# Router logits of the second mixture layer: tokens streamed over a stationary router, additions ahead of the turns, low parts behind the choice

## The chip, the cores and the metric

One Trainium2 chip, one of its cores. The time is that of one execution on the device in microseconds, the median of several runs. The core has TensorE (matmuls, "PE" in the rows, with its weight loads as "PEld"), VectorE ("DVE"), ScalarE ("ACT"), GpSimd ("POOL") and SyncE ("SP", which issues the DMAs here).

## What is computed

Two layers of a transformer over 512 tokens of width 1024. Layer 0 is attention and a mixture of experts, layer 1 a pooling mixer and a mixture of experts; a last norm ends it. The change lies between the pooling mixer of layer 1 and its mixture. There the reference does, in float32:

```python
x_lat = x_lat + g_m * pool_mixer(h_l, ...)          # four channel groups of 256, windows 2, 4, 8, 16
tokens = modulate(rms_norm(x_lat, norm_ffn_g[i]), sh_f, sc_f)
pg = softmax(tokens @ w_rg)                          # 4 groups
le = tokens @ w_re                                   # 32 experts, 8 of them per group
grp = top_k(pg, 1); two experts = top_k(le of that group, 2)
y = for each chosen expert: (silu(h @ w_gate) * (h @ w_up)) @ w_down, weighted and summed per token
```

So each token needs 36 logits (4 + 32), a choice from them, its rank among the tokens of its expert, and then the experts' products, two experts (a pair) at a time, for which 16 pairs of weights of 12 MB each are streamed from HBM.

## The kernel before, in words

Tokens lie on partitions, in NT = 4 tiles of 128; `x(j)` is token tile j, 1024 channels wide, or 8 chunks of 128 channels (k = 0 to 7). The program fixes the order of every engine's instructions by the order in which the code issues them; a tile pool adds the waits when a buffer is used again. PSUM is handed out by tags: one bank each for "g", "u", "t" and "ga", two for "y" and two for "c"; the router's bias takes a "y" bank, the logits bank `self.lg` the "ga" bank.

`pool_layer` (L1680) does the pooling. For each channel group g of 256 channels (two chunks), `project(g, tags)` (L1756) multiplies the pooled differences by the group's weights: 16 matmuls of TensorE into two banks. `added(g, ps)` (L1770) adds each bank to `x` on VectorE (two token tiles at once) and then squares the sums on ScalarE, one activation with a running sum for each token tile. When a chunk k of `x` is final, `turn(k, tag, eng)` (L1782) transposes it: four transposes on TensorE into a PSUM bank, then a copy into `xT` by ScalarE or VectorE. The chunks that are final first are turned first: 0, 1 (group 0), 6, 7 (group 3), 4, 5 (group 2) and 2, 3 (group 1).

`logits(*ks)` (L1791) multiplies the turned chunks by the router. The turned 128 tokens are the stationary operand, 128 columns of the router (36 of them the chunk's logits, the rest what lies behind) the moving one: four products per chunk, 32 in all, which add up in the bank `self.lg`. A matmul with zeros opens that bank.

The norm's factor r is not needed for the products: `add_shift` (L1180) multiplies the logits by r and adds the bias `bw`. It comes from `ss`, the 16 sums of squares per token: a sum, `rstd_of` (L501: a square root on ScalarE and five small steps on VectorE, with a place for other work between them, the argument `fill`). With r, `norm_high` (L1161) writes the rounded half `hi` of a normed token tile on ScalarE, and `norm_low` (L1169) the rest `lo` on VectorE, in two pieces for each token tile j, one for the even and one for the odd chunks.

Behind the logits stand `choose` (L1198, some 24 small VectorE steps that end in the table `M`), on TensorE meanwhile `row_bcast` (L477) and `zeros` (L1337, 20 matmuls with zeros that open four banks), then `rank` (L1239), `one_hot_tile` (L1552, the table `OH` of slots for token tile j) and `gather_part` (L1344), which for a pair of chunks and some token tiles multiplies `hi` and `lo` (parts 0 and 1) by `OH`: 64 matmuls altogether. ScalarE and VectorE evict them into `xe` (L1353). Then every engine passes a branch (`overflow`, L1495: taken if an expert has more tokens than it has slots), and the mixture runs (`moe`, L1563), pair after pair. Its weights come through `Stream` (L117), a ring of 12 buffers that `fill` issues on SP and `done` gives back.

Of the kernel before, what the change touches and what calls it, by code (L numbers as in the profile page):

```python
# [11 lines left out]
F32 = mybir.dt.float32  # L12
# [4 lines left out]
ALU = mybir.AluOpType  # L17
AX = mybir.AxisListType.X
PSUM = bass.MemoryType.PSUM

D = 1024
KD = D // 128
SEQ = 512
NT = SEQ // 128
# [3 lines left out]
HD = 64  # L28
# [4 lines left out]
NE = 32  # L33
NG = 4
# [5 lines left out]
UNIT = 64  # L40
# [26 lines left out]
_C = {}  # L67
_off = 0
for _n, _w in (("ident", 128), ("iota", SEQ), ("tcol", NT), ("w8", EPG), ("w4", NG),
               ("islot", UNIT), ("edge", 4 * 16), ("tri", 128), ("cos", NT * HD), ("sin", NT * HD),  # L70
               ("band", sum(WB for WB in BANDS.values()))):
    _C[_n] = (_off, _off + _w)
    _off += _w
# [3 lines left out]
def make_consts():  # L77
    c = np.zeros((128, NCONST), np.float32)

    def put(n, v):  # L80
        a, b = _C[n]
        c[:, a:b] = v

    p = np.arange(128)
    put("ident", np.eye(128))
    put("tri", p[:, None] < p[None, :])
    put("iota", np.arange(SEQ)[None] + 1)

    put("islot", np.where(np.arange(UNIT) < CAP, np.arange(UNIT) + 1, 0.5)[None])
    put("tcol", p[:, None] + 128 * np.arange(NT)[None] + 1)  # L90
    put("w8", EPG - np.arange(EPG)[None])
    put("w4", NG - np.arange(NG)[None])
    t = np.r_[np.arange(8), np.arange(SEQ - 8, SEQ)]
    edge = [np.float32(w) / (np.minimum(t + w // 2, SEQ) - np.maximum(t - w // 2, 0)).astype(np.float32) for w in WINDOWS]
    put("edge", np.concatenate(edge)[None])
    nf = HD // 4
    inv = (np.float32(10000.0) ** (-np.arange(nf, dtype=np.float32) / np.float32(nf))).astype(np.float32)
    tok = np.arange(SEQ)
    ang = np.concatenate([(tok // GRID_W).astype(np.float32)[:, None] * inv,
                          (tok % GRID_W).astype(np.float32)[:, None] * inv], axis=1).astype(np.float32)  # L100
    cs = np.repeat(np.cos(ang), 2, axis=1).reshape(NT, 128, HD).transpose(1, 0, 2)
    sn = np.sin(ang)
    sn = np.stack([-sn, sn], axis=-1).reshape(NT, 128, HD).transpose(1, 0, 2)
    bands = []
    for w, z in BANDS:
        tile = (0, 1, NT - 1)[z]
        src = 128 * tile + np.arange(128)[:, None]
        t = max(0, 128 * tile - w // 2 + 1) + np.arange(BANDS[w, z])[None]
        lo, hi = np.maximum(t - w // 2, 0), np.minimum(t + w // 2, SEQ)
        bands.append(((src >= lo) & (src < hi)) * (np.float32(1) / (hi - lo).astype(np.float32)))  # L110
    put("band", np.concatenate(bands, axis=1))
    put("cos", cs.reshape(128, -1))
    put("sin", sn.reshape(128, -1))
    return c
# [82 lines left out]
class Kernel:  # L197
# [47 lines left out]
    def load_consts(self):  # L245
        nc, a, cp = self.nc, self.a, self.cp
        ca = _C["edge"][1]
        self.cst = cp.tile([128, ca], F32, name="cst")
        rows = self.rowsA = cp.tile([96, 128], F32, name="rowsA")
        nc.sync.dma_start(self.cst[:, :128], a["consts"][:, :128])  # L250
        for i, n in enumerate(("c", "c_ctx")):
            nc.sync.dma_start(rows[8 * i:8 * i + 8], a[n].rearrange("(k p) -> k p", p=128))
        self.xc = self.big([128, NC_, D], F32, "xc")
        nc.sync.dma_start(self.xc, a["ctx"].rearrange("(j p) d -> p j d", p=128))
        nc.sync.dma_start(rows[16:32], a["norm_mix_g"].rearrange("i (k p) -> (i k) p", p=128))
        nc.sync.dma_start(rows[32:48], a["norm_ffn_g"].rearrange("i (k p) -> (i k) p", p=128))
        nc.sync.dma_start(rows[48:96], a["b_ada"][0].rearrange("(k p) -> k p", p=128))
        g = lambda n: self.cst[:, _C[n][0]:_C[n][1]]
        self.ident, self.iota, self.islot = g("ident"), g("iota"), g("islot")
        self.tcol, self.w8, self.w4, self.edge = g("tcol"), g("w8"), g("w4"), g("edge")  # L260
        self.tri_b = cp.tile([128, 128], BF16, name="tri_b")
        self.ones_b = cp.tile([128, 128], BF16, name="ones_b")
        nc.vector.memset(self.ones_b, 1.0)
        self.ones = cp.tile([128, 32], F32, name="ones")
        nc.vector.memset(self.ones, 1.0)

        self.cols = cp.tile([128, 144], F32, name="cols")

        self.AB = {}

        self.AB2 = {}

        self.gates = cp.tile([128, 512], F32, name="gates")
        nc.gpsimd.memset(self.gates, 0.0)
# [1405 lines left out]
    def pool_layer(self, norms):  # L1680
        nc, mp, pm, st, sm, pw = self.nc, self.mp, self.pm, self.st, self.sm, self.pw
# [6 lines left out]
        zero = self.tri_b[:, 0:1].to_broadcast([128, 128]), self.ones_b[:, 0:1].to_broadcast([128, 512])  # L1688
# [67 lines left out]
        def project(g, tags):  # L1756

            ps = []
            for jj in range(2):
                p = pm.tile([128, 2, 256], F32, tag=tags[jj], name="pp")  # L1760
                for j in range(2):
                    for z in range(2):
                        nc.tensor.matmul(p[:, j], diff[2 * g + z][:, (2 * jj + j) * 128:(2 * jj + j + 1) * 128],
                                         pw[:, 2 * g + z], start=(z == 0), stop=(z == 1))
                ps.append(p)
            return g, ps

        ss = sm.tile([128, NT, 4], F32, name="ss16")

        def added(g, ps):  # L1770

            q = slice(g * 256, (g + 1) * 256)
            for jj in range(2):
                xs = self.xt[jj][:, :, q]
                nc.vector.tensor_add(xs, xs, ps[jj])
                for j in (2 * jj, 2 * jj + 1):
                    junk = mp.tile([128, 256], F32, name="act")
                    nc.scalar.activation(junk, self.x(j)[:, q], AF.Square, accum_out=ss[:, j, g:g + 1])

        xT = []  # L1780

        def turn(k, tag, eng):  # L1782

            if not xT:
                xT.extend(self.big([128, 4, 512], F32, "xT") for _ in range(2))
            p = pm.tile([128, 512], F32, tag=tag, name="pb")
            for j in range(NT):
                nc.tensor.transpose(p[:, j * 128:(j + 1) * 128], self.x(j)[:, k * 128:(k + 1) * 128], self.ident)
            (nc.scalar.copy if eng is nc.scalar else nc.vector.tensor_copy)(xT[k // 4][:, k % 4], p)

        def logits(*ks):  # L1791

            for k in ks:
                for j in range(NT):
                    nc.tensor.matmul(self.lg[:, j * 128:(j + 1) * 128], xT[k // 4][:, k % 4, j * 128:(j + 1) * 128], self.wr(k),
                                     start=False, stop=(k == 3 and j == NT - 1))

        for js in (range(2), range(2, NT)):
            for k in (0, 1, 6, 7):
# [29 lines left out]
        summed(3)  # L1829
        self.router(1, self.gw[:, 1])  # L1830
        self.norm_begin()
        nc.tensor.matmul(self.lg, *zero, start=True, stop=False)
        p2 = project(2, ("t", "y"))
        added(*p3)
        turn(0, "c", nc.scalar)
        turn(1, "c", nc.scalar)
        p1 = project(1, ("g", "u"))
        added(*p2)
        turn(6, "y", nc.scalar)
        turn(7, "c", nc.vector)  # L1840
        added(*p1)
        turn(4, "y", nc.vector)
        turn(5, "c", nc.vector)
        logits(0, 1, 6, 7)
        st4 = sm.tile([128, NT], F32, name="ss4")
        nc.vector.tensor_reduce(st4, ss, axis=AX, op=ALU.add)
        r = self.rstd_of(st4, NT, D, "n4")
        hl = {}

        def high(j):  # L1850
            hl[j] = self.norm_high(j, r[:, j:j + 1])

        def low(j, k):
            self.norm_low(j, r[:, j:j + 1], *hl[j], k)

        turn(2, "y", nc.vector)
        turn(3, "c", nc.scalar)
        high(0)
        high(1)
        logits(4, 5, 2, 3)  # L1860
        low(0, 0)
        low(0, 1)
        low(1, 0)
        low(1, 1)
        self.route_begin()
        for j in range(NT):
            self.add_shift(j, r[:, j:j + 1])
# [10 lines left out]
        OH = mp.tile([128, NT, 4 * CAP], F32R, name="OH")  # L1878
        for j in range(2):
            self.one_hot_tile(OH, 0, j)  # L1880
        self.fullest_of()
        for j in range(2, NT):
            self.one_hot_tile(OH, 0, j)
# [1 line left out]
                low(j, k)  # L1885
        self.spread_two()
        xe = self.slots_tile()
        for js in (range(2), range(2, 3)):
            for k in range(0, KD, 2):
                self.gather_part(OH, k, js)  # L1890
        self.tc.mark_branch_hint_location("over1", engines=(mybir.EngineType.PE,))
        for k in range(0, KD, 2):
            self.gather_part(OH, k, range(3, 4))
# [67 lines left out]
```

## Time and profile before

| what | value |
|---|---|
| median of 3 runs | 1376.76 us (1374.62 to 1382.63) |
| the profiled execution, its own time | 1378.12 us |
| its span, from the first to the last instruction | 1376.3 us |
| mean granted clock of TensorE | 0.987 of full speed |
| PE, DVE, ACT busy over the span | 96%, 48%, 26% |
| bytes read from HBM | 472.51 MB, 345 GB/s over the span |

The times in the rows are microseconds from the span's first instruction. Shares of busy time over the whole span say little here, since the change touches some 25 of 1376 us; the rows below are of that stretch, of the stretch behind it, and of a few other places where something alike was done.

### The profile page before, as it was taken

To read this page: it belongs to the slowest core of one execution; us is meant where nothing else is said; L and a number is where in the kernel's file an instruction comes from. 1 tells how busy PE (TensorE), PEld (TensorE's weight loads), DVE (VectorE), ACT (ScalarE), POOL (GpSimd) and SP (SyncE) were. 2 spreads that over 40 slices of the span, in tenths; PEclk is the share of its full clock that TensorE was granted. 3 is DMA by queue.
4 is the path that set the end of the run, shared out by engine and by line. 5 is a ranking of instruction groups with operands and counts; after the bars stand their busy time and mean duration, and the time that the engine had idled before them with its cause. 6 is when DMAs were issued, how large, how long until landed. Compare 5 with 4: busy or idle time off the path is not lost. (4 is left out here: it accounts for less than half of the span.)

```text
span 1376.3 us, 18679 instructions
## 1 busy us (share of the span) xinstructions
PE 1314.4 (96%) x7191; PEld 736.4 (54%) x7191; DVE 659.7 (48%) x1290; ACT 363.7 (26%) x707; POOL 130.2 (9%) x130
## 2 busy tenths in 40 slices
PE   3799999999999999999999999999999999999995
PEld 1578677778744544445444435754455444554442
DVE  2778788867823434234342335744234342343335
ACT  2554687763311111111111105521111111111103
POOL 1523344340000000000000010000000000000001
PEclk9799999999999999999999999999999999999998
DMA  9411846159489999999999999579999999999994
GB/s 373 171 62 62 337 142 227 40 197 361 191 365 426 427 426 427 426 427 426 426 427 426 422 411 423 225 292 411 426 426 427 425 427 426 427 426 426 427 420 172
DMA packets 80704, 475.91 MB, mean 346 GB/s; under 512 B 8512, under 2 KB 10064, under 8 KB 30432
## 3 DMA queue, kind: packets, MB, share of 16 engines
q1 hardware_dynamic: 80600, 474.64, 84.0%
q8 instruction: 58, 0.95, 0.3%
q14 instruction: 38, 0.31, 0.1%
q10 hardware_dynamic: 8, 0.01, 0.0%
HBM read 472.51 MB, written 2.11 MB: 345 GB/s over the span
## 5 line engine op out<-in xcount | busy, mean ns | idle before, releaser
L1371 PE MATMUL pgate<-wt,xe 128*64 128x512 f32 x1024 | 273.1, 593 | 2.7 <-ACTq L1504 2.1
L1371 PE MATMUL pup<-wt,xe 128*64 128x512 f32 x1024 | 271.8, 592 | 0.3 <-DVEq L1504 0.3
L1396 PE MATMUL py<-wt,aT 128*64 128x512 f32 x960 | 212.6, 595 | 0.0
L1376 DVE TENSOR_TENSOR act<-act,pup 128x512 f32<-128x512 f32 x32 | 22.0, 689 | 342.8 <-ACT act L1375 310.5
L1427 DVE TENSOR_TENSOR x<-x,pc 128x512 f32<-128x512 f32 x240 | 154.1, 683 | 29.9 <-PE pc L1425 29.9
L1371 PEld LDWEIGHTS pgate<-wt,xe 128*64 128x64 f32 x1024 | 75.8, 137 | 148.5 <-issue 129.5
L1371 PEld LDWEIGHTS pup<-wt,xe 128*64 128x64 f32 x1024 | 76.5, 137 | 145.5 <-issue 143.2
L1425 PE MATMUL pc<-y,scat 128*128 128x512 f32 x480 | 136.7, 406 | 2.4 <-DVE x L1427 2.4
L1409 DVE SCALAR_TENSOR_TENSOR py<-py,r_sw,gw 128x512 f32<-128x512 f32 x64 | 48.6, 759 | 178.4 <-PE py L1396 169.5
L1396 PEld LDWEIGHTS py<-wt,aT 128*64 128x64 f32 x960 | 66.9, 137 | 124.0 <-issue 118.8
L1325 PE MATMUL pga<-OH,xnp 128*128 128x224 f32 x896 | 119.3, 277 | 0.0
L1325 PEld LDWEIGHTS pga<-OH,xnp 128*128 128x128 f32 x896 | 114.3, 191 | 8.5 <-issue 1.6
L1375 ACT ACTIVATE act<-pgate 128x512 f32<-128x512 f32 x32 | 19.1, 597 | 360.8 <-PE pgate L1371 348.4
L1425 PEld LDWEIGHTS pc<-y,scat 128*128 128x128 f32 x480 | 80.3, 189 | 42.8 <-ACT act L1375 24.3
L1410 ACT ACTIVATE y<-py 128x512 fp32r<-128x512 f32 x64 | 38.1, 596 | 235.3 <-PE py L1396 160.1
L1334 POOL MEMSET xe<- 128x64 f32 x16 | 2.4, 151 | 781.6 <-PE pup L1371 551.3
L1360 ACT ACTIVATE xe<-pga,mod 128x224 f32<-128x224 f32 x64 | 33.8, 538 | 154.8 <-PE pga L1325 139.6
L562 PE MATMUL pmm<-whl,hT 128*128 128x512 f32 x288 | 70.6, 402 | 0.0
L850 DVE TENSOR_REDUCE mx<-S 128x1 f32<-128x768 f32 x64 | 58.3, 951 | 19.5 <-PE S L847 18.9
L562 PEld LDWEIGHTS pmm<-whl,hT 128*128 128x128 f32 x288 | 54.6, 193 | 11.3
L857 ACT ACTIVATE P<-S,mx 128x768 f32<-128x768 f32 x64 | 56.9, 899 | 2.2 <-POOL rest L731 2.1
L867 PE MATMUL PT<-cst,P 128*128 128x128 f32 x384 | 54.5, 277 | 0.1
(345 smaller groups left out, 1414.7 us busy)
## 6 DMA issues: line engine op xcount, KB each, us to landing
wt<-in_moe_w_gate_up_dram SPq DMA_DIRECT2D x224, 1024.0 KB
wt<-in_moe_w_down_dram SPq DMA_DIRECT2D x120, 1024.0 KB
wt<-in_w_ada_dram SPq DMA_DIRECT2D x48, 1024.0 KB
wt<-in_moe_w_gate_up_dram SPq DMA_DIRECT2D x64, 512.0 KB
wt<-in_moe_w_down_dram SPq DMA_DIRECT2D x16, 512.0 KB
wt<-in_attn_w_qkv_dram SPq DMA_DIRECT2D x6, 1024.0 KB
x<-in_x_dram SPq DMA_DIRECT2D x8, 512.0 KB
wt<-in_attn_w_o_dram SPq DMA_DIRECT2D x4, 1024.0 KB
```

The costliest lines, as they stand in the source:

```text
L562: self.nc.tensor.matmul(p, lhs(pa, k), whl[pb, k // 4][:, k % 4], start=(k + n == 0), stop=(k == KD - 1 and n == 2))
L850: nc.vector.tensor_reduce(m, s[:, :NKEY], axis=AX, op=ALU.max, negate=True)
L857: nc.scalar.activation(P[n][:, g], S.pop((n, g))[:, :NKEY], AF.Exp, bias=mx[n, g], accum_out=total[n // 4][:, 2 * gp + g, kvl:kvl + 1])
L867: nc.tensor.transpose(pt[:, cc, g * 128:(g + 1) * 128], P[n][:, g, c * 128:(c + 1) * 128], self.ident)
L1325: nc.tensor.matmul(p[:, :n], self.parts[part][j // 2][:, j % 2, k * 128:(k + 1) * 128], OH[:, j], start=(z == 0), stop=(z == 2 * NT - 1))
L1360: nc.scalar.activation(xe, p, AF.Identity, bias=B[:, k:k + 1], scale=A[:, k:k + 1])
L1371: nc.tensor.matmul(p[64 * e:64 * e + 64], xe(k)[:, offs[e]:offs[e] + UNIT], w[e][:, h * 512:(h + 1) * 512], start=(k == 0), stop=(k == KD ...
L1396: nc.tensor.matmul(py[h][64 * e:64 * e + 64], aT[:, j, 64 * e:64 * e + 64], wd[e][:, h * 512:(h + 1) * 512], start=(j == 0), stop=(j == 3) ...
L1409: nc.vector.scalar_tensor_tensor(py, py, w, gf[:, h * 512:(h + 1) * 512], op0=ALU.mult, op1=ALU.mult)
L1410: nc.scalar.activation(y[:, 0], py, AF.Copy)
L1425: nc.tensor.matmul(p, P[:, j * 128:(j + 1) * 128], y[:, part], start=(part == 0), stop=(part == 1))
L1427: nc.vector.tensor_add(xs, xs, p)
```

## The change: what it does

1. **Logits turned round.** The router's columns of a chunk (64 of them, 36 used) become the stationary operand, the 512 turned tokens the moving one. Even chunks go to the lower 64 columns of the array and to partitions 0 to 63 of one PSUM bank, odd chunks to the upper 64 and partitions 64 to 127: 8 products of 64x512. The bank then holds two halves of the sum, turned. `logits_end` copies it to SBUF (VectorE) and multiplies each 128 tokens of it by a constant table `halves` (a 1 where p mod 64 is the column), which turns it back and adds the halves: four products of 128x36 into `self.lg`. The matmul with zeros goes. The constants grow by 36 columns.
2. **Banks.** The bank of those halves is "t", so group 2's projection takes ("y", "y") in place of ("t", "y").
3. **Additions first.** Group 1's additions (`added(*p1)`) stand ahead of the turns of chunks 6 and 7, and the sum of squares and the norm's factor ahead of chunks 4 and 5, whose turns and the first logits are the work inside `rstd_of`. Copies change engine: 6 and 2 and 7 by VectorE, 4, 5 and 3 by ScalarE. `high(0)` stands ahead of the turns of 2 and 3.
4. **Low parts behind the choice.** Of the four `low` pieces of token tiles 0 and 1 that stood ahead of the choice one stays, behind `logits_end`; three go behind the first two `one_hot_tile`. The gather of token tiles 0 and 1 takes part 0 for all chunks first, and then part 1.

```diff
         def logits(*ks):
             for k in ks:
-                for j in range(NT):
-                    nc.tensor.matmul(self.lg[:, j * 128:(j + 1) * 128], xT[k // 4][:, k % 4, j * 128:(j + 1) * 128], self.wr(k),
-                                     start=False, stop=(k == 3 and j == NT - 1))
+                q = slice(k % 2 * 64, k % 2 * 64 + 64)
+                nc.tensor.matmul(lgT[0][q], self.wr(k)[:, :64], xT[k // 4][:, k % 4], start=(k < 2), stop=(k in (2, 3)),
+                                 tile_position=(0, k % 2 * 64))
+
+        def logits_end():
+            t = mp.tile([128, 512], F32, tag="aT", name="lgT")
+            nc.vector.tensor_copy(t, lgT[0])
+            for j in range(NT):
+                nc.tensor.matmul(self.lg[:, j * 128:j * 128 + NG + NE], t[:, j * 128:(j + 1) * 128], self.halves, start=True, stop=True)
...
-        nc.tensor.matmul(self.lg, *zero, start=True, stop=False)
-        p2 = project(2, ("t", "y"))
+        lgT.append(pm.tile([128, 512], F32, tag="t", name="lgT"))
+        p2 = project(2, ("y", "y"))
         added(*p3)
         turn(0, "c", nc.scalar)
         turn(1, "c", nc.scalar)
         p1 = project(1, ("g", "u"))
         added(*p2)
-        turn(6, "y", nc.scalar)
+        added(*p1)
+        turn(6, "y", nc.vector)
         turn(7, "c", nc.vector)
-        added(*p1)
-        turn(4, "y", nc.vector)
-        turn(5, "c", nc.vector)
-        logits(0, 1, 6, 7)
         st4 = sm.tile([128, NT], F32, name="ss4")
-        nc.vector.tensor_reduce(st4, ss, axis=AX, op=ALU.add)
-        r = self.rstd_of(st4, NT, D, "n4")
...
+        nc.vector.tensor_reduce(st4, ss, axis=AX, op=ALU.add)
+
+        def meanwhile():
+            turn(4, "y", nc.scalar)
+            turn(5, "c", nc.scalar)
+            logits(0, 1, 6, 7)
+
+        r = self.rstd_of(st4, NT, D, "n4", meanwhile)
+        high(0)
         turn(2, "y", nc.vector)
         turn(3, "c", nc.scalar)
-        high(0)
         high(1)
         logits(4, 5, 2, 3)
+        logits_end()
         low(0, 0)
-        low(0, 1)
-        low(1, 0)
-        low(1, 1)
+        lows = [(0, 1), (1, 0), (1, 1)]
         self.route_begin()
...
         for j in range(2):
             self.one_hot_tile(OH, 0, j)
+        for z in lows:
+            low(*z)
         self.fullest_of()
...
-        for js in (range(2), range(2, 3)):
+        for js, parts in ((range(2), (0,)), (range(2), (1,)), (range(2, 3), range(2))):
             for k in range(0, KD, 2):
-                self.gather_part(OH, k, js)
+                self.gather_part(OH, k, js, parts)
```

The order of the instructions at three places, as the two programs issue them. A row holds the line, the operation, what it writes and reads, and the shape; the changed program's line numbers are 2 to 20 higher.

**TensorE, from group 2's projection to the broadcast of the gate row, before.** (`pp` are projections, `pb<-cst,x` transposes, `pb<-gw,xT` logits, `pb<-gates` the broadcast.)

```order
L1763 MATMUL pp<-pw,phm 128x256 x8
L1788 MATMUL pb<-cst,x 128x128 x8
L1763 MATMUL pp<-pw,pab 128x256 x8
L1788 MATMUL pb<-cst,x 128x128 x16
L1795 MATMUL pb<-gw,xT 128x128 x16
L1788 MATMUL pb<-cst,x 128x128 x8
L1795 MATMUL pb<-gw,xT 128x128 x16
L483 MATMUL pb<-gates,cst 128x512 x2
```

The same place in the changed program:

```order
L1765 MATMUL pp<-pw,phm 128x256 x8
L1790 MATMUL pb<-cst,x 128x128 x8
L1765 MATMUL pp<-pw,pab 128x256 x8
L1790 MATMUL pb<-cst,x 128x128 x16
L1798 MATMUL lgT<-xT,gw 64x512 x4
L1790 MATMUL pb<-cst,x 128x128 x8
L1798 MATMUL lgT<-xT,gw 64x512 x4
L1806 MATMUL pb<-cst,lgT 128x36 x4
L485 MATMUL pb<-gates,cst 128x512 x2
```

The places of the two groups of logits stay; 16 products become 4 in each, and the four products that sum the halves stand between the last of them and the broadcast.

**VectorE and ScalarE, from group 1's additions to the scaled logits, before.** VectorE's twelve rows, then ScalarE's (`act,ss` are the squares, `xnp` the high parts on ScalarE and the low parts on VectorE, `n4` the norm's factor):

```order
L1775 TENSOR_TENSOR x<-x,pp 128x2x256 x2
L1789 COPY xT<-pb 128x512 x2
L1846 TENSOR_REDUCE ss_7107<-ss_6812 128x4
L505 TENSOR_SCALAR n4v<-ss_7107 128x4
L510 RECIPROCAL n4r<-n4r 128x4
L512 TENSOR_TENSOR n4t<-n4r 128x4
L513 TENSOR_TENSOR n4t<-n4t,n4v 128x4
L514 TENSOR_SCALAR n4t<-n4t 128x4
L515 TENSOR_TENSOR n4r<-n4r,n4t 128x4
L1789 COPY xT<-pb 128x512
L1170 SCALAR_TENSOR_TENSOR xnp<-x,n4r,xnp 128x4x128 x4
L1181 SCALAR_TENSOR_TENSOR L<-pb,n4r,bw 128x36 x4
```

```order
L1778 ACTIVATE act,ss_6812<-x 128x256 x4
L1789 COPY xT<-pb 128x512
L1778 ACTIVATE act,ss_6812<-x 128x256 x4
L507 ACTIVATE n4r<-n4v 128x4
L1789 COPY xT<-pb 128x512
L1166 ACTIVATE xnp<-x,n4r 128x1024 x2
L484 COPY gw<-pb 128x512 x2
```

The same in the changed program, VectorE (its first row holds the additions of groups 3, 2 and 1; the row behind the last one is `L<-pb,n4r,bw` again) and ScalarE:

```order
L1777 TENSOR_TENSOR x<-x,pp 128x2x256 x6
L1791 COPY xT<-pb 128x512 x2
L1863 TENSOR_REDUCE ss_7079<-ss_6812 128x4
L507 TENSOR_SCALAR n4v<-ss_7079 128x4
L512 RECIPROCAL n4r<-n4r 128x4
L514 TENSOR_TENSOR n4t<-n4r 128x4
L515 TENSOR_TENSOR n4t<-n4t,n4v 128x4
L516 TENSOR_SCALAR n4t<-n4t 128x4
L517 TENSOR_TENSOR n4r<-n4r,n4t 128x4
L1791 COPY xT<-pb 128x512
L1804 COPY lgT<-lgT 128x512
L1172 SCALAR_TENSOR_TENSOR xnp<-x,n4r,xnp 128x4x128
```

```order
L1780 ACTIVATE act,ss_6812<-x 128x256 x8
L509 ACTIVATE n4r<-n4v 128x4
L1791 COPY xT<-pb 128x512 x2
L1168 ACTIVATE xnp<-x,n4r 128x1024
L1791 COPY xT<-pb 128x512
L1168 ACTIVATE xnp<-x,n4r 128x1024
L486 COPY gw<-pb 128x512 x2
```

On VectorE no copy stands between the additions any more, and one low part in place of four ahead of the scaled logits. On ScalarE no copy stands between the squares, two copies follow the root, and the copy of chunk 3 stands behind the first high part.

**VectorE, from the ranks to the last low parts, before.** (`OH` are the tables of slots.)

```order
L1248 SCALAR_TENSOR_TENSOR r_rk<-pr,r_M 128x128
L1553 TENSOR_TENSOR OH<-cst,r_rk 128x224 x2
L1256 TENSOR_REDUCE r_fullest<-pr 128x1
L1553 TENSOR_TENSOR OH<-cst,r_rk 128x224
L1170 SCALAR_TENSOR_TENSOR xnp<-x,n4r,xnp 128x4x128 x2
L1553 TENSOR_TENSOR OH<-cst,r_rk 128x224
L1170 SCALAR_TENSOR_TENSOR xnp<-x,n4r,xnp 128x4x128 x2
```

And in the changed program:

```order
L1250 SCALAR_TENSOR_TENSOR r_rk<-pr,r_M 128x128
L1555 TENSOR_TENSOR OH<-cst,r_rk 128x224 x2
L1172 SCALAR_TENSOR_TENSOR xnp<-x,n4r,xnp 128x4x128 x3
L1258 TENSOR_REDUCE r_fullest<-pr 128x1
L1555 TENSOR_TENSOR OH<-cst,r_rk 128x224
L1172 SCALAR_TENSOR_TENSOR xnp<-x,n4r,xnp 128x4x128 x2
L1555 TENSOR_TENSOR OH<-cst,r_rk 128x224
L1172 SCALAR_TENSOR_TENSOR xnp<-x,n4r,xnp 128x4x128 x2
```

Three low parts now stand between the second table and everything behind it on VectorE.

## Rows read from the trace of the kernel before

**Rows 1.** Busy time of the engines in two stretches: from the end of the weights' ring being filled to the next weight DMA, and from there nearly to the end. Columns: stretch, its length, then busy us (and instructions) of PE, PEld, DVE, ACT and POOL, PE's granted clock, the DMA engines' share, GB/s.

```profile
879.00:902.60 23.60, 21.08 (x160) 16.52 (x161) 17.04 (x61) 9.84 (x17) 0.00 (x0) 1.00 0.03 12
902.60:1350.00 447.40, 445.16 (x2263) 211.63 (x2261) 162.39 (x294) 53.45 (x93) 1.06 (x7) 1.00 1.01 421
```

**Rows 2.** The instructions of SP's queue in order of time, from 860 to 925 us: start, length, what, and how many. The first row is the last group ahead of the gap.

```profile
862.36 4.01 SPq L136 DMA_DIRECT2D wt<-in_moe_w_down_dram  x4
902.64 12.57 SPq L136 DMA_DIRECT2D wt<-in_moe_w_gate_up_dram  x8
```

**Rows 3.** The waits of TensorE's matmuls from 920 us to the end, the longest first: who waited for whom, us in total, times, longest.

```profile
PE pc L1456 <- ACT y L1410: 1.7, 1, 1.7
```

**Rows 4.** TensorE in order of time, merged: start, length until the last matmul is drained, line, what, count; in brackets the idle time before it and what ended it. A float32 matmul of the program counts twice here, a transpose once. Several rows are left out.

```profile
866.48 0.65 PE L1147 MATMUL pb<-mod,cst 128*64 128x4 f32 x16
...
867.29 3.62 PE L1763 MATMUL pp<-pw,phm 128*128 128x256 f32 x16
870.74 1.04 PE L1788 MATMUL pb<-cst,x 128*128 128x128 f32 x8
871.62 3.62 PE L1763 MATMUL pp<-pw,pab 128*128 128x256 f32 x16
875.07 1.91 PE L1788 MATMUL pb<-cst,x 128*128 128x128 f32 x16
876.82 3.74 PE L1795 MATMUL pb<-gw,xT 128*128 128x128 f32 x32
...
881.27 3.74 PE L1795 MATMUL pb<-gw,xT 128*128 128x128 f32 x32
884.84 1.88 PE L483 MATMUL pb<-gates,cst 128*128 128x512 f32 x4
886.56 4.54 PE L1341 MATMUL pga<-ones_b,tri_b 128*128 128x512 bf16 x20
892.14 0.18 PE L1244 MATMUL pr<-r_M,tri_b 128*128 128x32 bf16 x1 [1.05 <-DVE r_M L1235]
...
893.45 7.46 PE L1349 MATMUL pga<-OH,xnp 128*128 128x224 f32 x64 [0.27 <-DVE OH L1553]
901.73 1.08 PE L1371 MATMUL pgate<-wt,xe 128*64 128x512 f32 x4 [0.82 <-ACTq L1504]
```

**Rows 5.** VectorE in order of time, the same columns, several rows left out.

```profile
868.96 0.18 DVE L1152 COPY bw<-pb 128x36 f32<-128x36 f32 x1
...
869.42 2.48 DVE L1775 TENSOR_TENSOR x<-x,pp 128x512 f32<-128x512 f32 x4
876.15 0.69 DVE L1789 COPY xT<-pb 128x512 f32<-128x512 f32 x1 [4.25 <-PE pb L1788]
876.75 1.27 DVE L1775 TENSOR_TENSOR x<-x,pp 128x512 f32<-128x512 f32 x2
877.95 1.28 DVE L1789 COPY xT<-pb 128x512 f32<-128x512 f32 x2
879.69 0.17 DVE L1846 TENSOR_REDUCE ss<-ss 128x4 f32<-128x16 f32 x1 [0.46 <-ACT act L1778]
...
881.15 0.16 DVE L515 TENSOR_TENSOR n4r<-n4r,n4t 128x4 f32<-128x4 f32 x1
...
883.22 2.74 DVE L1170 SCALAR_TENSOR_TENSOR xnp<-x,n4r,xnp 128x512 fp32r<-128x512 f32 x4 [1.31 <-ACT xnp L1166]
885.88 0.73 DVE L1181 SCALAR_TENSOR_TENSOR L<-pb,n4r,bw 128x36 f32<-128x36 f32 x4
...
892.91 0.69 DVE L1553 TENSOR_TENSOR OH<-cst,r_rk 128x224 fp32r<-128x224 f32 x2
...
893.92 1.41 DVE L1170 SCALAR_TENSOR_TENSOR xnp<-x,n4r,xnp 128x512 fp32r<-128x512 f32 x2
```

**Rows 6.** ScalarE in order of time, the same columns: the end of the last square of group 2, the first and the last of group 1's, the copy of chunk 3, and the high parts of token tiles 0 and 1.

```profile
875.13 0.19 ACT L1778 ACTIVATION_READ_ACCUMULATOR act<-x 128x1 f32 x1
...
877.52 0.42 ACT L1778 ACTIVATE act<-x 128x256 f32<-128x256 f32 x1 [1.23 <-DVE x L1775]
...
879.47 0.19 ACT L1778 ACTIVATION_READ_ACCUMULATOR act<-x 128x1 f32 x1
...
881.47 0.58 ACT L1789 COPY xT<-pb 128x512 f32<-128x512 f32 x1 [1.16 <-PE pb L1788]
881.95 2.40 ACT L1166 ACTIVATE xnp<-x,n4r 128x1024 fp32r<-128x1024 f32 x2
```

**Rows 7.** The chain of work that ended last, at the start of layer 1's mixture: start, length, what. The first row is a product with a stationary operand 128 columns wide, the others are products of two experts with 64 columns each, at the lower and the upper half of the array, four instructions for one chunk of both experts.

```profile
908.16 0.65 PE pw L1308 x4
908.81 1.01 PE pgate L1371 x4
909.82 0.86 PE pup L1371 x4
```

**Rows 8.** Busy time and granted clock (columns as in rows 1) of two stretches near the start of the kernel, and of two around the choice.

```profile
65.00:70.00 5.00, 3.27 (x15) 2.38 (x13) 4.42 (x10) 0.75 (x3) 4.96 (x9) 1.00 0.00 0
70.00:75.00 5.00, 3.27 (x13) 2.73 (x14) 3.90 (x13) 3.40 (x10) 0.03 (x1) 0.54 0.02 5
890.00:892.50 2.50, 1.45 (x16) 0.72 (x14) 1.88 (x10) 0.00 (x0) 0.00 (x0) 1.00 0.00 0
892.50:895.00 2.50, 1.85 (x19) 1.72 (x17) 2.38 (x7) 0.00 (x0) 0.00 (x0) 1.00 0.03 7
```

More of the change, by code (lines that the diff above doesn't have):

```diff
@@ L69 @@
 for _n, _w in (("ident", 128), ("iota", SEQ), ("tcol", NT), ("w8", EPG), ("w4", NG),
-               ("islot", UNIT), ("edge", 4 * 16), ("tri", 128), ("cos", NT * HD), ("sin", NT * HD),
+               ("islot", UNIT), ("halves", NG + NE), ("edge", 4 * 16), ("tri", 128), ("cos", NT * HD), ("sin", NT * HD),
                ("band", sum(WB for WB in BANDS.values()))):
@@ L89, in make_consts @@
     put("islot", np.where(np.arange(UNIT) < CAP, np.arange(UNIT) + 1, 0.5)[None])
+    put("halves", p[:, None] % 64 == np.arange(NG + NE)[None])
     put("tcol", p[:, None] + 128 * np.arange(NT)[None] + 1)
@@ L258, in load_consts @@
         g = lambda n: self.cst[:, _C[n][0]:_C[n][1]]
-        self.ident, self.iota, self.islot = g("ident"), g("iota"), g("islot")
+        self.ident, self.iota, self.islot, self.halves = g("ident"), g("iota"), g("islot"), g("halves")
         self.tcol, self.w8, self.w4, self.edge = g("tcol"), g("w8"), g("w4"), g("edge")
@@ L1793, in logits @@
             for k in ks:
-                for j in range(NT):
-                    nc.tensor.matmul(self.lg[:, j * 128:(j + 1) * 128], xT[k // 4][:, k % 4, j * 128:(j + 1) * 128], self.wr(k),
-                                     start=False, stop=(k == 3 and j == NT - 1))
+                q = slice(k % 2 * 64, k % 2 * 64 + 64)
[6 more added lines that the diff above has]
+                nc.tensor.matmul(self.lg[:, j * 128:j * 128 + NG + NE], t[:, j * 128:(j + 1) * 128], self.halves, start=True, stop=True)
+        lgT = []
         for js in (range(2), range(2, NT)):
```

## The prediction

> **What bounds the kernel.** I read the stretches first. From 879 to 902.6 us the DMA engines carry almost nothing (share 0.03), since the ring of weights is full; from 902.6 on they run at a share of 1.01 while TensorE is busy for 445 of 447 us [rows 1]. So the kernel's last third starts with the mixture of layer 1, and the question is when. SP's queue shows it: its next weight DMA goes out at 902.64, just behind TensorE's first product of the mixture at 901.73 [rows 2, 4]. From 920 us on the longest wait of TensorE's matmuls altogether is 1.7 us, on ScalarE in the tail [rows 3]: the mixture goes at TensorE's pace. Both TensorE's start and the DMAs' hang on the same stretch, so an earlier start by some time should end the kernel earlier by that time. The change has to be costed on the chain that leads to 901.73.
>
> That chain, read backwards in the orders of time: the gather takes 893.45 to 900.7 without a gap on TensorE (64 instructions, 0.113 us apart) [rows 4]; it needs the first tables, which need the ranks, and those the table M, for which TensorE waited 1.05 us before 892.14 [rows 4]. M is the end of some 24 short VectorE steps behind the scaled logits at 885.88 [rows 5]. There two things come together. TensorE's logits end as its next product starts, at 884.84 [rows 4], and are readable about 0.2 us later; but VectorE was at four low parts until 885.9 [rows 5]. Those needed the high parts (from 881.95), these the norm's factor (done at 881.3), this the last square (879.66) [rows 5, 6]. And the squares of group 1 began only at 877.52, because VectorE had stood idle for 4.25 us until chunk 7 was turned, had copied it, and only then had added group 1 (876.75 to 878.0) [rows 5, 6]. The projection it adds was done when TensorE went on at 875.07 [rows 4].
>
> **Additions first.** The second half of group 2's projection takes the "y" bank that the router's bias leaves at 869.14 [rows 5]; from 867.29 at 0.215 us an instruction it would start at 869.0, or at 868.8 without the matmul of zeros that goes. It starts at about 869.2, and what follows on TensorE is 0.2 us later: group 1's projection ends at 875.3. VectorE, now with nothing between, adds its second bank by 876.1 (0.62 us each) [rows 5], then copies 6 and 7 by 877.4, which nothing waits for yet. ScalarE is done with group 2's squares at 875.32 [rows 6]; a square takes (879.66 - 877.52)/4 = 0.54 us [rows 6], the third can start at 876.4, the last ends at 877.5. From the sum of squares to the factor took 881.31 - 879.69 = 1.62 us [rows 5], so the factor is there at 879.17 instead of 881.31: **2.1 us** earlier.
>
> **Logits turned round.** A group of 16 products took from 881.27 to 884.84, 3.57 us [rows 4]. The nearest row for the new form is the mixture's own: two float32 products with 64 columns each, at the two halves of the array, over 512 moving columns, take 0.86 us together [rows 7]. Two such pairs make 1.72 us. Changing between whole and halved stationary operands shows in the same rows: the first such product behind one of 128 columns took 1.01 instead of 0.86 us [rows 7], so I put 0.15 us on each change. Chunks 0, 1, 6, 7 then go from 877.0 to 878.9, the turns of 2 and 3 to 879.9 (eight transposes in 0.88 us [rows 4], and a change). ScalarE copies 4 and 5 behind the root by 879.25, writes the first high part (half of 2.40 us [rows 6]) from 879.25 to 880.45, and only then copies chunk 3, by 881.05: what was late by the norm is late by this copy now. Chunks 4, 5 go from 880.05 to 880.9, 2 and 3 from 881.05 to 881.9.
>
> **What the turning adds.** The copy of the halves: 0.2 us until TensorE's result is readable and 0.69 us for 128x512 on VectorE [rows 5], to 882.8. Four summing products, eight instructions: no row has this form. As 128 columns are loaded for each, the nearest is a transpose, 0.11 us an instruction [rows 4]: 0.9 us; the lower bound is 0.04 us, from the products of 4 columns (0.65 us for 16 [rows 4]): 0.3 us. I take 0.9, and 0.15 for a change: to 883.85, readable at 884.0. The one low part that stays (0.7 us) lies beside them. The scaled logits start at 884.0 instead of 885.88: **1.9 us** earlier, and M with them, since the choice is untouched: 890.2.
>
> TensorE must be free by then. Behind the summing products it has the broadcast (884.84 to 886.56, 1.72 us) and the 20 matmuls of zeros (886.56 to about 891.05, 4.5 us) [rows 4]: from 883.85 to 890.1. It just makes it; before, it was idle for 1.05 us here. So this cover is gone: from here on whatever delays the logits on TensorE also delays the ranks.
>
> [...]
>
> **Low parts behind the choice.** Three of them, 0.69 us each [rows 5], follow the second table, 2.05 us. The gather starts as before with part 0 of the first two token tiles: 16 instructions at 0.113 us, 1.8 us. Part 1 begins with what is written already; only its fourth instruction needs the last low part, some 0.1 us late. The tables and low parts of token tiles 2 and 3 come 2.05 us later on VectorE, but TensorE reaches them after 16 more instructions each, 3.6 and 5.4 us into the gather, with 2.6 + 1.4 and 2.6 + 1.4 + 1.7 us of VectorE's work ahead of their last piece: again 0.1 to 0.3 us at most, some of it the same wait. I take 0.1. The count of the fullest expert also comes 2 us later, and the engines read it only at the gather's end. The 36 more columns of constants load long before; they cost nothing that the first stretch of the kernel would show.
>
> **The sum.** 1.9 - 0.1 = 1.8 us. The profiled execution (1378.12 us by its own time, 1376.3 by its span) would become 1376.3 us; it lies 1.4 us above the median of 1376.76, from which I forecast **1375.0 us**. The gain's bounds: at most 3.0 (no late bank, 0.2; no switches, 0.3; cheap summing, 0.6; no stall, 0.1), at least 0.3 (first rival).
>
> **The rivals.**
> 1. *The halves don't run side by side.* The mixture's four instructions come as two experts of one chunk, with both halves fed in turn for hundreds of microseconds; here the pairs are short, and chunk 3's half starts when its copy comes. One after the other, each pair costs 0.86 us more. Chunk 5 ends at 881.75, chunk 3 at 883.45, 1.55 us later, all of it on the chain. The gain shrinks to 0.3 us: 1376.5. For it: no row shows so short a group; against it: rows 7 show the same shapes overlapping from their first pair on.
> 2. *The end doesn't follow the start.* The DMA share of 1.01 [rows 1] could mean that the weights decide and not TensorE. Against it: hardly a wait of TensorE, and the DMAs restart with the same event. For it to hold, the DMAs would have to be paced by something outside this stretch. Then 1376.8, no change: the kernel's logits get shorter and its time doesn't.
> 3. *TensorE's clock falls, slower than before.* A stretch with TensorE busy for 3.27 of 5 us near the start was followed by one at 0.54 of full speed; around the choice it was busy for 1.45 + 1.85 = 3.3 of 5 us, and the clock stayed at 1.00 [rows 8]. So the old order was no further from a fall than that one. The change adds a hole of 0.9 us while VectorE copies the halves, and takes away one of 1.05. [...]
>
> **How the numbers follow.** Forecast, a gain between 1.0 and 3.0: 0.66. Halves one after the other: 0.18. End doesn't follow: 0.10. Clock: 0.06. The three runs lie 2.1 below and 5.9 above their median, and a median moves by perhaps half of that. The range goes from the lowest run less the largest gain, 1374.62 - 3.0 = 1371.6, to the first rival with half of the upper spread, 1376.5 + 2.9 = 1379.4; the fallen clock is left out. A change of 0.5%, 6.9 us, is about what a measurement of this kernel can tell from none. No case gains that: the whole stretch from the last additions to the mixture is 26 us. I leave 0.04 to it for the runs' own spread, 0.04 to slower (the fallen clock together with a high run, above 1383.6), and 0.92 to no change.
>
> **What would show it.** In the new profile: group 1's last square ends about 2 us earlier against the end of its projection; each later group of logits takes under 2 us of TensorE; chunk 3's copy ends last before them; VectorE's scaled logits start some 8.7 us behind the end of group 1's projection instead of 10.8; TensorE's idle time before the ranks is near zero; the gather's 64 instructions still take about 7.3 us; the mixture starts by 1.8 us earlier against the same point, and from there on all is as it was. The forecast is wrong if a pair of halves takes 1.7 us, if the gather has holes of over 0.5 us, if the clock in this stretch is below 1.00, or if the mixture's length changes.

## The result and the profile after

The changed kernel takes 1388.45 us (median of 6 runs, 1386.11 to 1390.15), the kernel before in the same comparison 1378.09 us (6 runs, 1374.62 to 1382.63): a ratio of 1.008, interval 1.0064 to 1.0095. That is **10.4 us slower**, where 1.8 us faster was forecast. The profiled execution took 1389.41 us, its span 1387.6.

The stretch on which the whole prediction was spent did what was forecast. TensorE from group 1's projection to the mixture, columns as in [rows 4]:

```profile
878.89 3.62 PE L1765 MATMUL pp<-pw,pab 128*128 128x256 f32 x16
882.34 1.91 PE L1790 MATMUL pb<-cst,x 128*128 128x128 f32 x16
884.18 1.94 PE L1798 MATMUL lgT<-xT,gw 128*64 128x512 f32 x8
886.05 1.09 PE L1790 MATMUL pb<-cst,x 128*128 128x128 f32 x8
887.07 1.94 PE L1798 MATMUL lgT<-xT,gw 128*64 128x512 f32 x8
889.83 1.08 PE L1806 MATMUL pb<-cst,lgT 128*128 128x36 f32 x8 [0.82 <-DVE lgT L1804]
890.74 1.96 PE L485 MATMUL pb<-gates,cst 128*128 128x512 f32 x4
892.54 4.54 PE L1343 MATMUL pga<-ones_b,tri_b 128*128 128x512 bf16 x20
897.22 0.19 PE L1246 MATMUL pr<-r_M,tri_b 128*128 128x32 bf16 x1
...
898.44 7.66 PE L1351 MATMUL pga<-OH,xnp 128*128 128x224 f32 x64 [0.18 <-DVE OH L1555]
906.93 1.08 PE L1373 MATMUL pgate<-wt,xe 128*64 128x512 f32 x4 [0.83 <-ACTq L1506]
```

VectorE, as in [rows 5]:

```profile
885.90 0.16 DVE L517 TENSOR_TENSOR n4r<-n4r,n4t 128x4 f32<-128x4 f32 x1
...
889.09 0.69 DVE L1804 COPY lgT<-lgT 128x512 f32<-128x512 f32 x1 [1.65 <-PE lgT L1798]
890.95 0.74 DVE L1183 SCALAR_TENSOR_TENSOR L<-pb,n4r,bw 128x36 f32<-128x36 f32 x4 [0.52 <-PE pb L1806]
```

But all of it lies late. A mark ahead of every edit is the start of group 0's projection, before and after:

```profile
856.39 3.61 PE L1763 MATMUL pp<-pw,pab 128*128 128x256 f32 x16
```

```profile
863.32 3.61 PE L1765 MATMUL pp<-pw,pab 128*128 128x256 f32 x16
```

It comes 6.93 us later. From it to the mixture's first product the kernel before took 901.73 - 856.39 = 45.34 us, this one 906.93 - 863.32 = 43.61: the stage gained **1.73 us**. From there to the span's end it took 1387.6 - 906.9 = 480.7 us against 1376.3 - 901.7 = 474.6: 6.1 us lost. So 6.9 - 1.7 + 6.1 = 11.3 us, the difference of the spans of these two executions, and both losses lie where no line of the diff stands: in and about the mixtures. What differs there is the rate of the DMAs. The same 300 us in the middle of layer 1's mixture (columns as in [rows 1]; the last is GB/s), before and after:

```profile
1000.00:1300.00 300.00, 300.00 (x1558) 148.05 (x1556) 111.89 (x191) 36.49 (x64) 0.76 (x5) 1.00 1.01 427
```

```profile
1000.00:1300.00 300.00, 298.67 (x1523) 143.22 (x1520) 107.00 (x183) 35.43 (x62) 0.76 (x5) 1.00 1.01 421
```

The DMA engines are as full as before, and move 1.4% less. From 400 to 800 us, in layer 0's mixture, the rate is 424 GB/s before and 420 after. Whether that costs time shows in the pace of the pairs. TensorE's turn of the activations comes once for each pair; two pieces of the mixture, before:

```profile
1064.21 0.60 PE L1383 MATMUL paT<-cst,act 128*128 128x128 f32 x4
1092.86 0.60 PE L1383 MATMUL paT<-cst,act 128*128 128x128 f32 x4
...
1207.44 0.60 PE L1383 MATMUL paT<-cst,act 128*128 128x128 f32 x4
1236.09 0.60 PE L1383 MATMUL paT<-cst,act 128*128 128x128 f32 x4
1264.73 0.60 PE L1383 MATMUL paT<-cst,act 128*128 128x128 f32 x4
1294.02 0.60 PE L1383 MATMUL paT<-cst,act 128*128 128x128 f32 x4
```

and after:

```profile
1069.36 0.60 PE L1385 MATMUL paT<-cst,act 128*128 128x128 f32 x4
1098.00 0.60 PE L1385 MATMUL paT<-cst,act 128*128 128x128 f32 x4
...
1214.12 0.60 PE L1385 MATMUL paT<-cst,act 128*128 128x128 f32 x4
1243.88 0.60 PE L1385 MATMUL paT<-cst,act 128*128 128x128 f32 x4
1273.88 0.60 PE L1385 MATMUL paT<-cst,act 128*128 128x128 f32 x4
```

In the first piece a pair takes 28.65 us in both: TensorE's pace. In the second it still does before, up to a last step of 29.29 us, but after it takes 29.8 and 30.0 us: the weights' pace, since 12.6 MB at 421 GB/s are 29.9 us. The chain of waits of that stretch (start, length, what) alternates between weights on their way, some 20 us, and some 10 us of TensorE, left out here:

```profile
1183.39 20.64 DMA wt<-in_moe_w_gate_up_dram
...
1214.02 19.80 DMA wt<-in_moe_w_gate_up_dram
```

Even at 427 GB/s a pair's weights need 29.5 us, 0.8 us more than TensorE; the full ring at the mixture's start is a lead that pays for that, up to the step of 29.29 us, the thirteenth. At 421 GB/s the weights fall behind by 1.2 us in each pair, and the lead is gone after ten.

TensorE's waits in the mixture show it only in part. The gate products' waits for their weights from 907 us on (us in total, times, longest) are, before, one row, of the weight loads:

```profile
PEld pgate L1371 <- DMA wt<-in_moe_w_gate_up_dram: 1.1, 2, 0.6
```

and after two, one of the matmuls and one of the weight loads:

```profile
PE pgate L1373 <- DMA wt<-in_moe_w_gate_up_dram: 1.4, 4, 0.5
...
PEld pgate L1373 <- DMA wt<-in_moe_w_gate_up_dram: 7.0, 9, 1.4
```

Even in the changed kernel, whose mixture lost 6.1 us, the matmuls themselves wait 1.4 us for these weights.

### The profile page after: what moved, and what is told of

Read it like the earlier page. It is cut to its first block, busy times and chain, and to the rows that moved or that the text cites. A ratio compares the mean times of both kernels' runs of the same rounds, so it can differ in the third digit from the quotient of the medians.

```text
span 1387.6 us, 18595 instructions
## 1 busy us (share of the span) xinstructions
PE 1324.4 (95%) x7150; PEld 731.9 (53%) x7150; DVE 659.9 (48%) x1290; ACT 364.1 (26%) x708; POOL 130.2 (9%) x130
## 5 line engine op out<-in xcount | busy, mean ns | idle before, releaser
L1373 PE MATMUL pgate<-wt,xe 128*64 128x512 f32 x1024 | 286.4, 594 | 5.1 <-DMA wt<-in_moe_w_gate_up_dram 2.4
L1373 PE MATMUL pup<-wt,xe 128*64 128x512 f32 x1024 | 283.5, 593 | 0.3 <-DVEq L1506 0.3
L1373 PEld LDWEIGHTS pgate<-wt,xe 128*64 128x64 f32 x1024 | 78.6, 137 | 158.7 <-issue 128.6
L1373 PEld LDWEIGHTS pup<-wt,xe 128*64 128x64 f32 x1024 | 79.3, 137 | 146.2 <-issue 144.0
```

What stands on the lines that cost most here:

```text
L1373: nc.tensor.matmul(p[64 * e:64 * e + 64], xe(k)[:, offs[e]:offs[e] + UNIT], w[e][:, h * 512:(h + 1) * 512], start=(k == 0), stop=(k == KD ...
```

## The experiments

Why would the DMAs slow down, when SP's queue holds the same transfers in the same order? One thing in the diff reaches them: the 36 columns of `halves` make the tile of constants 144 bytes per partition longer, rounded to 160, and everything that SBUF holds behind it moves up. One of the weight buffers starts at byte 104192 before and at 104352 after. All buffers of the ring lie 8192 bytes or multiples of it apart, so they share one remainder: 0 modulo 256 before, 160 after. There are three explanations. **Theory S**: the start of the weight buffers in SBUF sets the rate. **Theory D**: the wider table of constants in HBM does. **Theory C**: the new order of instructions does.

**pad160_before.** The kernel before, one line more:

```diff
         rows = self.rowsA = cp.tile([96, 128], F32, name="rowsA")
+        cp.tile([128, 40], F32, name="pad")
```

> The kernel before with one unused tile of 160 bytes per partition behind the constants, and nothing else: every weight buffer of the ring starts 160 bytes higher in SBUF, at the very addresses that it has in the changed kernel (104192 becomes 104352 for the first, which is 0 and 160 modulo 256). Theory S, the start of the weight buffers in SBUF slows every weight DMA: weights at 421 GB/s in mid-mixture instead of 427, and slower than the kernel before by what the changed kernel lost plus what its stage gained, 10.4 + 1.7 = about 12 us, 1390 us. Theory D, the wider table of constants in HBM does it: 427 GB/s and 1378 us. Theory C, the new order of instructions does it: 427 GB/s and 1378 us.

Measured: 1389.51 us against 1377.06, ratio 1.0096 (1.007 to 1.0121), and in mid-mixture

```profile
1000.00:1300.00 300.00, 299.56 (x1528) 144.34 (x1525) 108.15 (x185) 35.67 (x62) 0.76 (x5) 1.00 1.01 421
```

A tile that nothing reads or writes costs 12.4 us, about what the changed kernel lost and its stage gained together (10.4 + 1.7). C and D fall, since this kernel has neither the new order nor the wider table.

**after_halves64.** The changed kernel with the table padded:

```diff
-               ("islot", UNIT), ("halves", NG + NE), ("edge", 4 * 16), ...
+               ("islot", UNIT), ("halves", 64), ("edge", 4 * 16), ...
...
-                nc.tensor.matmul(..., t[:, j * 128:(j + 1) * 128], self.halves, start=True, stop=True)
+                nc.tensor.matmul(..., t[:, j * 128:(j + 1) * 128], self.halves[:, :NG + NE], start=True, stop=True)
```

> The changed kernel with the table of halves 64 columns wide instead of 36, of which 36 are used: the weight buffers start 256 bytes higher than before, again at a multiple of 256. Theory S: 427 GB/s, and the gain of the stage shows in the end, 1378.1 - 1.7 = about 1376.4 us. Theory D (the table in HBM is wider still): 421 GB/s and about 1388 us. Theory C: 421 GB/s and about 1388 us.

Measured: 1375.12 us (12 runs, 1374.36 to 1376.28) against 1377.06, ratio 0.998 (0.9969 to 0.9992); 426 GB/s; 43.62 us from the mark to the mixture. With the buffers back at a multiple of 256 the change is worth 1.9 us (by the interval 1.1 to 4.3), which agrees with the 1.7 that the stage gained.

**wide_consts_before.** `("spare", 36)` added at the end of the table in HBM, never loaded.

> The kernel before with 36 more columns at the end of the table of constants in HBM, never loaded: all SBUF addresses as before, the table's rows as long as in the changed kernel. Theory S: 427 GB/s and 1378 us. Theory D: 421 GB/s and about 1390 us. Theory C: 1378 us.

Measured: 1377.22 us, ratio 1.0003 (0.999 to 1.0016), 426 GB/s. The wider table in HBM alone costs nothing, which speaks against D a second time.

**pad64_before, pad128_before, pad256_before.** The pad of the first experiment with 16, 32 and 64 columns.

> The kernel before with an unused tile of 64 bytes per partition: the weight buffers start at 64 modulo 256. Theory S with a bound of 64 bytes or less: 427 GB/s and 1378 us. Theory S with a bound of 256 bytes: 421 GB/s or so, and about 1390 us. Theories D and C: 1378 us.

> The kernel before with an unused tile of 128 bytes per partition: the weight buffers start at 128 modulo 256 in SBUF. If what the weight DMAs need is a start at a multiple of 256 bytes: 421 GB/s in mid-mixture, ratio 1.008 to 1.010, about 1389 us. If 128 bytes do: 427 GB/s and 1377 us.

> The kernel before with an unused tile of 256 bytes per partition: the weight buffers start at a multiple of 512 in SBUF (before: 256 modulo 512). If a multiple of 256 is enough: 427 GB/s and no change, 1377 us. If the DMAs gain from 512: above 427 GB/s, and up to the stretch in which TensorE is the bound, faster. If any shift of the buffers costs: about 1389 us.

| pad | start of the buffers modulo 256 | GB/s in mid-mixture | us | ratio (interval) |
|---|---|---|---|---|
| 64 bytes | 64 | 421 | 1389.32 | 1.008 (1.0058 to 1.0103) |
| 128 bytes | 128 | 421 | 1391.19 | 1.0101 (1.007 to 1.0133) |
| 160 bytes | 160 | 421 | 1389.51 | 1.0096 (1.007 to 1.0121) |
| 256 bytes | 0 | 426 | 1376.54 | 0.9997 (0.9982 to 1.0012) |

Three different offsets lose the same; a whole 256 loses nothing, and a start at a multiple of 512 gains nothing (426 GB/s). From 427 GB/s in the kernel before to 421 is 1.4%, for 64, 128 and 160 bytes alike.

**after_spare96.** The pads so far moved constants and small tiles too. Here the changed kernel keeps them where it has them and gets its ring back:

```diff
+            pool(es, "spare").tile([128, 24], F32, name="pad")
             self.s8 = pool(es, "s8", S8_SLOTS)
```

> The changed kernel as it is, its table of halves 36 wide, with one unused tile of 96 bytes per partition between the small tiles and the ring of weight buffers: the constants and the small tiles keep the addresses of the changed kernel, the weight buffers (and what lies above them) start at a multiple of 256 again. If the weight buffers' start is the cause: 427 GB/s and, with the stage's gain, 1375 us, ratio 0.998. If the moved constants or small tiles are the cause: 421 GB/s and 1388 us.

Measured: 1375.58 us (12 runs) against 1377.36, ratio 0.9984 (0.9972 to 0.9996).

```profile
1000.00:1300.00 300.00, 300.00 (x1558) 147.22 (x1558) 111.24 (x191) 36.67 (x64) 0.76 (x5) 1.00 1.01 426
```

So it is the ring (with what lies above it), and 96 unused bytes turn the change from 10 us slower to 1.8 us faster. This version and after_halves64 can't be told apart.

The profiled executions agree with one another. In the ten whose ring starts at a multiple of 256 the mark lies at 854.1 to 857.5 us and the time from the mixture's first product to the end is 473.6 to 475.9 us; in the four whose ring does not, the changed kernel among them, it is 860.7 to 866.0 and 479.4 to 480.7 us. So the 6.9 us ahead of the stage are the figure of one pair of executions, and the figures for the others spread by a few us.

**The parts of the stage.** Five kernels take the change apart, each measured from the mark to the mixture's first product: 45.34 us before, 43.62 with all parts (after_halves64). Each was profiled once, but the stage repeats well: four further executions of the old order with the clock up took 45.34 to 45.37 us, and the three of the whole change 43.61 to 43.63. Two kernels leave a part out of after_halves64: low_ahead puts back the four `low` calls ahead of `route_begin` and the old loop of the gather; old_logits puts back the 32 products, the zeros and the banks ("t", "y").

> The changed kernel with the table of halves 64 wide, and the low parts and the gather as before: all four low parts of token tiles 0 and 1 ahead of the scaled logits. From the start of group 0's projection to the first product of the mixture the kernel before took 45.3 us and the changed one 43.6. If moving the low parts carries a part of the gain: the scaled logits wait for VectorE, 3 x 0.69 less what the summing products covered, 1.5 us later, the gather 0.2 shorter: 44.9 us. If the gain is all of the additions and the turned logits: 43.6.

> The changed kernel with the table of halves 64 wide (unused here), the additions first and the low parts behind the choice, but the logits as before, 32 products with the tokens stationary. From the start of group 0's projection to the first product of the mixture: if the turned logits carry their part of the gain, two groups of 3.57 us instead of 1.9, less the copy and the summing products: 1.4 us later than the changed kernel, 45.0 us. If turning them costs as much as it saves: 43.6.

Three add one part to the kernel before: turned_only the new `logits`, `logits_end` and banks; low_behind_only the moved `low` calls and the gather by parts; additions_first_only the order of `added`, `turn`, `rstd_of` and `high(0)`.

> The kernel before with the turned logits alone (table of halves 64 wide): additions, copies and low parts in the old order. From the start of group 0's projection to the first product of the mixture, 45.3 us before: the norm's factor comes as late as before, the copy of the halves joins the four low parts on VectorE, the scaled logits start at about 886.4 instead of 885.9: 45.9 us, slower. If the logits were the bound before: 44 us or less.

> The kernel before with three low parts behind the choice and the gather of token tiles 0 and 1 by parts, all else as before. The scaled logits then wait for TensorE's logits at 885.05 instead of VectorE at 885.9; the gather 0.2 us longer: 44.7 us instead of 45.3. If the low parts were covered: 45.3 or more.

> The kernel before with the additions, the norm's factor and the copies in the new order (table of halves 64 wide, unused), logits and low parts as before. The factor comes 2 us earlier and the low parts with it, but TensorE's logits end at 884.8 as before: the scaled logits at 885.05 instead of 885.9, 44.5 us instead of 45.3. If the factor alone was the bound: 43.3 us.

| kernel | expected | from the mark to the mixture | against before |
|---|---|---|---|
| low_behind_only | 44.7 | 901.17 - 856.54 = 44.63 | -0.71 |
| additions_first_only | 44.5 | 901.97 - 857.46 = 44.51 | -0.83 |
| turned_only | 45.9 | 901.82 - 855.63 = 46.19 | +0.85 |
| old_logits | 45.0 | 899.90 - 855.28 = 44.62 | -0.72 |
| low_ahead | 44.9 | 900.50 - 854.14 = 46.36 | +1.02 |
| all parts | | 43.62 | -1.72 |

The parts alone sum to -0.69, together they give -1.72. Turned logits alone lose, since the copy of the halves joins four low parts on VectorE: the scaled logits start 30.33 us behind the mark instead of 29.49. With the other two in place they gain 1.0 (old_logits against all parts). Additions and low parts together give no more than either alone (old_logits), since all three kernels then wait for the same logits: VectorE stands idle for 0.38 us (additions), 1.07 (low parts) and 2.66 (both) until TensorE's logits are there. low_ahead missed by 1.5 us, and its gather shows why. TensorE's rows, and the granted clock (columns as in [rows 8]):

```profile
889.43 0.19 PE L1246 MATMUL pr<-r_M,tri_b 128*128 128x32 bf16 x1 [1.53 <-DVE r_M L1237]
...
890.65 9.03 PE L1351 MATMUL pga<-OH,xnp 128*128 128x224 f32 x64 [0.18 <-DVE OH L1555]
```

```profile
887.50:890.00 2.50, 0.81 (x12) 0.34 (x11) 1.80 (x10) 0.00 (x0) 0.00 (x0) 1.00 0.00 0
890.00:892.50 2.50, 2.10 (x13) 2.00 (x13) 2.47 (x7) 0.00 (x0) 0.00 (x0) 0.64 0.00 0
892.50:895.00 2.50, 2.50 (x17) 2.50 (x17) 2.15 (x6) 0.00 (x0) 0.00 (x0) 0.68 0.01 3
```

TensorE stood idle for 1.53 us ahead of the ranks, and the clock fell in the gather: 9.03 us instead of 7.46. Without that fall the run would be at 44.8, as expected. Each of the five ran once, so their whole times (1375.73 to 1378.56 us) say nothing.

## Why the prediction was wrong

**The step that failed** is one sentence of the forecast: "The 36 more columns of constants load long before; they cost nothing that the first stretch of the kernel would show." It priced the columns as bytes to load. Their price is the address of all that lies behind them: 1.4% of the DMA rate, and through it 6.9 us ahead of the stage and 6.1 behind it in the profiled executions. With it fell the last expectation, "from there on all is as it was", and one of the forecast's own signs of being wrong came true: the mixture's length changed.

**The reading that made it possible** was "the mixture goes at TensorE's pace". For the trace of before that was right, as 28.65 us for each pair shows. But I took the absence of waits for room, and there was none: 1.01 of the DMA engines were in use [rows 1], and 12.6 MB at 427 GB/s are 29.5 us, more than TensorE's 28.65. Dividing a pair's bytes by the rate would have shown that the weights lose on TensorE in every pair and that only the ring's lead hides it. The list of the matmuls' waits [rows 3] could hardly have shown it: in the changed kernel, too, it has 1.4 us for the weights. The second rival held the doubt ("the weights decide and not TensorE"), but priced it at no change, since I saw nothing that would move the DMAs.

**The rest held**, but for the late bank, which cost 0.34 us (group 1's projection at 871.96 against 871.62) where 0.2 was forecast. Set back by the 6.93 us, the norm's factor was done at 879.13 (forecast 879.17); the first group of logits took 884.18 to 886.05, 1.87 us (1.72 and 0.15 for the change of width); the turns 1.02 (0.88 and 0.15); the copy of the halves began at 882.16 (882.1); the summing products took 0.91 (0.9); the scaled logits began at 884.02 (884.0); the ranks at 890.29 with TensorE just free (890.2); the gather took 0.2 us longer (0.1); the mixture began 1.73 earlier (1.8). The first rival is out: a group of two pairs took 1.87 us, where one half after the other would have taken 1.7 for each pair. The "no switches, 0.3" of the gain's upper bound are two such changes of width at 0.15 us; the 1.87 and 1.02 us agree with the 0.15, but no run has the turned logits without them. after_halves64, the change with the ring at a multiple of 256, gained 1.9 us where 1.8 was forecast. That its 1375.12 us lie so near to the forecast 1375.0 is in part luck, since the median of the kernel before moved between 1376.15 and 1378.09 us from one comparison to the next.

**The third rival**, the falling clock, did not come to pass in the changed kernel (granted 1.00 in every 2.5 us from 885 to 907.5), but it is real here. It came where TensorE waited 1.5 us for M (low_ahead) and once in pad128_before, whose order is that of before, with 1.06 us of waiting:

```profile
900.00:902.50 2.50, 1.10 (x14) 0.52 (x12) 1.82 (x10) 0.00 (x0) 0.00 (x0) 1.00 0.00 0
902.50:905.00 2.50, 2.19 (x14) 2.11 (x14) 2.48 (x7) 0.00 (x0) 0.00 (x0) 0.64 0.03 10
```

There the gather took 9.01 us. Five other executions of that order had waits of 1.04 to 1.07 us at the same place and a gather of 7.45 or 7.46 us, which in the kernel before is that of a granted clock of 1.00, so the length of the wait does not decide it alone. The old order thus fell in one of six profiled executions, and the price was 1.6 us, in the gather. The hole that the forecast named, while VectorE copies the halves, lies ahead of the broadcast and the zeros. In turned_only the clock did fall there, to 0.50 of full speed from 885 to 887.5 us: the broadcast took 3.64 us until drained instead of 1.88. That cost the stage nothing, since M still came last (written by 892.17, the ranks at 892.23). In no run did a fall cost the stage more than 1.6 us; slower, for which the forecast had 0.04 and named the fallen clock, came about without one. Whether the narrower spread of after_halves64 (1374.4 to 1376.3 us, against 1374.9 to 1382.5 for before beside it) comes from such falls was not tested.

## What to carry to other kernels

Before a new constant or tile is called free, look at the address of what lies behind it: a stream of weights that starts at a multiple of 256 bytes should be kept there, by a pad or by widths that are such multiples (here 426 to 427 GB/s there, 421 at the three offsets tried). Where an engine and the DMAs are both near full, divide bytes by rate for one round of the loop and compare it with the engine's own time; no waits may only mean that a prefetched lead still lasts, and here 1.4% of rate was then worth 12 us. And a forecast of a local change needs a mark ahead of it and one behind it, so that a shift from elsewhere is seen apart from the stage.

## What the runs showed that was not expected

- The rate of the weight DMAs depends on where their buffers start in SBUF: 426 to 427 GB/s at a multiple of 256 bytes, 421 at 64, 128 and 160 above one, the same for all three. The start of the data in HBM was not varied; whether the 1.4% arises in the writes to SBUF themselves or in their pairing with the reads stays open.
- 1.4% of DMA rate cost 0.8 to 1.0% of the whole time in a kernel whose trace showed TensorE as the bound.
- TensorE's clock fell to a mean of 0.64 of full speed in 2.5 us, right behind waits of 1.53 us (low_ahead) and 1.06 us (pad128_before) between small products. The order of before, with a wait of 1.04 to 1.07 us each time, ran five times with the clock up and once with it down; what decides between them stays open.
